# The first scale and shift on 32-column tiles of TensorE, the first norm's scaling and modulation on VectorE

## The chip, the cores and the metric

The program runs on one core of a Trainium2 chip. The metric is the device time of one execution in microseconds. Below, TensorE is PE in the rows (PEld its weight loads), VectorE is DVE, ScalarE is ACT, GpSimd is POOL and SyncE is SP.

## The reference

A two-layer trunk over x of 1024 rows (frames) by 1024 features. Each sub-layer is: RMS norm, adaLN shift and scale made from a vector c, the sub-layer, a gate from c, and the residual sum. Only the beginning matters here:

```python
def rmsnorm(x, w):
    xf = xf * lax.rsqrt(jnp.mean(xf * xf, axis=-1, keepdims=True) + RMS_EPS)
    return xf.astype(x.dtype) * w

def modulate(h, shift, scale):
    return h * (1.0 + scale[:, None, :]) + shift[:, None, :]

# shift, scale, gate (six of 1024 per layer) = silu(c) @ ada_w + ada_b
# layer 0: proj = modulate(rmsnorm(x), shift, scale) @ even_w_in  -> u, q, k, v
```

So before the first projection can start, two products of silu(c) (1024 values) with a 1024x1024 block of `ada_w` must be done, one for the scale and one for the shift.

## The kernel before, in words

The program is written with tile pools, and a scheduler sets the order in which each engine's instructions stand. Each engine then works through its own list from the top, and an instruction that waits holds up all that stand behind it. The parts that the change touches lie in the first 60 us of layer 0 (`even`):

- **Weights** come through `wload` (L74): one transfer of 1 MB into a tile `w` of 128x2048 floats, issued on SP's queue. At the start two rings of two such buffers each serve them, so a fifth load waits until a buffer has been read for the last time.
- **`ada`** (L142) makes one of the six vectors. It loads `ada_w` in four blocks of 256 columns (`h` = 0 to 3), each as eight slices of 128 rows (`k`). Normally VectorE multiplies each slice by its eight values of silu(c) and sums them: one TENSOR_SCALAR (L160) and seven SCALAR_TENSOR_TENSOR (L167) per block give `adacc`, 128x256. TensorE then sums over the partitions, with two matmuls per block against a column of ones (L179). For the first scale, block 2 goes to TensorE as it is: sixteen matmuls with one moving column (L177). VectorE adds the bias (L180), which ends the vector.
- **`norm_S`** (L189) normalizes two tiles of 128 rows at a time: ScalarE squares and sums (L124), VectorE and GpSimd make the reciprocal root (`rm` L131, `rs` L133), the engine `eng` scales the row tile (`xn`, L201), TensorE transposes it in 128x128 pieces (L106). For the first four tiles ScalarE copies the transposed pieces to `pre` (this is `qT`'s memory, L213), since scale and shift aren't there yet.
- **`modulate`** (L217) makes `hm` = x * scale + shift for two slices of features: ScalarE takes one (L223), the engine `eng` the other (L225). Then `split` (L136) makes the high part `hTh` on ScalarE and the rest `hTl` on VectorE (L138, L139). Eight such blocks cover the first 512 rows. They are followed by the other 512 rows, whose `hm` comes straight from PSUM, with VectorE for the second slice.
- **The projections** need for each weight block its own `split` into `wh` and `wl` (two halves each) and then run as three matmuls per product (L240 to L242). They begin when the first blocks of `hTh` are there.
- Behind them, VectorE works in the background on the vectors of the next sub-layers (`gate1` and so on) in the same way.

In the kernel before, `eng` is GpSimd for `xn` of all eight row tiles and for `hm` of the first eight blocks.

Of the kernel before, what the change touches and what calls it, by code (L numbers as in the profile page):

```python
# [9 lines left out]
FT = mybir.dt.float32  # L10
# [13 lines left out]
KD = D // 128  # L24
# [12 lines left out]
class Core:  # L37
# [42 lines left out]
    def consts(self):  # L80
        nc, c = self.nc, self.const
        ji = c.tile([128, 128], I32, name="ji")
        nc.gpsimd.iota(ji, pattern=[[1, 128]], base=0, channel_multiplier=-1)
        self.ident = c.tile([128, 128], FT, name="ident")
        nc.vector.tensor_scalar(self.ident, ji, 0.0, None, op0=OP.is_equal)
        self.ustrict = c.tile([128, 128], BF, name="ustrict")
        nc.vector.tensor_scalar(self.ustrict, ji, 0.0, None, op0=OP.is_gt)
        self.ones_b = c.tile([128, 128], BF, name="ones_b")
        nc.vector.memset(self.ones_b, 1.0)
        self.ones_f = c.tile([128, 128], FT, name="ones_f")  # L90
        nc.vector.memset(self.ones_f, 1.0)
        self.nhalf = c.tile([128, 16], FT, name="nhalf")
        nc.vector.memset(self.nhalf, -0.5)
        self.euler = c.tile([128, 4], FT, name="euler")
        nc.vector.memset(self.euler, math.e)
        self.eps = c.tile([128, 1], FT, name="eps")
        nc.vector.memset(self.eps, 1e-6)
        cr = c.tile([128, KD], FT, name="cr")
        nc.sync.dma_start(cr, self.a["c"][0].rearrange("(k p) -> p k", p=128))
        self.cs = c.tile([128, KD], FT, name="cs")  # L100
        nc.scalar.activation(self.cs, cr, AF.Silu)
        self.mod_d = self.dram.tile([2, 6, D], FT, name="mod_d")
        self.mod = {}
# [37 lines left out]

    def ada(self, i, names, pool, tag, on_pe=((),), pool_eng=False):  # L142

# [3 lines left out]
        for m, nm in enumerate(names):  # L147
# [5 lines left out]
            for h in range(4):  # L153
                w = self.wload(aw[i, :, j * D + h * 256:j * D + (h + 1) * 256], 8)
                if h in on_pe[m % len(on_pe)]:
                    parts.append(w)
                    continue
# [13 lines left out]
            for h, x in enumerate(parts):  # L171
                for q in range(2):
                    qs = slice(q * 128, (q + 1) * 128)
                    p = pc[:, 2 * h + q:2 * h + q + 1]
                    if h in on_pe[m % len(on_pe)]:
                        for k in range(KD):
                            nc.tensor.matmul(p, x[:, k, qs], self.cs[:, k:k + 1], start=(k == 0), stop=(k == KD - 1))  # L177
                    else:
                        nc.tensor.matmul(p, x[:, qs], self.ones_f[:, 0:1], start=True, stop=True)  # L179
            nc.vector.tensor_tensor(o, pc[:, 0:KD], b, op=OP.add)  # L180
# [1804 lines left out]
    def even(self, x_src):  # L1985
# [9 lines left out]
        with self.banks("pse", b=4, a=1, d=1, e=2):  # L1995
# [16 lines left out]
            with tc.tile_pool(name="hT", bufs=1, side="right") as hp, tc.tile_pool(name="wsp", bufs=1, side="right") as wp:  # L2012
                hs = [hp.tile([128, KD, T], FR, name=n) for n in ("hTh", "hTl")]
                with tc.tile_pool(name="nrm", bufs=1, side="left") as np_:
# [13 lines left out]
                    pre = qT[:].rearrange("p h t -> p (h t)").rearrange("p (k t) -> p k t", k=KD)  # L2028
                    self.norm_S(get, None, None, *hs, np_, "ad", range(4), eng=nc.gpsimd, pre=pre)
                    list(self.ada(0, ["scale1", "shift1"], ap, "e", ((2,), ())))  # L2030
                    mod = self.mod["scale1", 0], self.mod["shift1", 0]
                    for h in range(2):
                        ts = slice(256 * h, 256 * h + 256)
                        for k in range(0, KD, 2):
                            self.modulate(pre[:, k:k + 2, ts], k, ts, *mod, *hs, np_, nc.gpsimd)
                    self.norm_S(get, *mod, *hs, np_, "ad", range(4, 8), 512, eng=nc.gpsimd)
                kv = pool(left, "kv", "left")
# [157 lines left out]
```

## Time and profile before

| | us |
|---|---|
| median of 3 runs (3063.31 to 3076.72) | 3067.4 |
| the profiled execution | 3067.3 |
| its span in the trace | 3065.6 |
| around the span | 1.7 |
| TensorE busy | 2658.0 (87%) |
| VectorE busy | 1790.3 (58%) |
| ScalarE busy | 1125.4 (37%) |
| GpSimd busy | 834.4 (27%) |

The shares are means over many stages. What the change is worth is read from the stretch that it touches: the opening up to the first projection at 60 us, the projections up to 288 us that follow it, and what waits for their end.

### The profile page before, as it was taken

To read this page: it belongs to the slowest core of one execution; us is meant where nothing else is said; L and a number is where in the kernel's file an instruction comes from. 1 tells how busy PE (TensorE), PEld (TensorE's weight loads), DVE (VectorE), ACT (ScalarE), POOL (GpSimd) and SP (SyncE) were. 2 spreads that over 40 slices of the span, in tenths; PEclk is the share of its full clock that TensorE was granted. 3 is DMA by queue.
4 is the path that set the end of the run, shared out by engine and by line. 5 is a ranking of instruction groups with operands and counts; after the bars stand their busy time and mean duration, and the time that the engine had idled before them with its cause. 6 is when DMAs were issued, how large, how long until landed. Compare 5 with 4: busy or idle time off the path is not lost. (4 is left out here: it accounts for less than half of the span.)

```text
span 3065.6 us, 39902 instructions
## 1 busy us (share of the span) xinstructions
PE 2658.0 (87%) x14357; PEld 1855.2 (61%) x14357; DVE 1790.3 (58%) x3207; ACT 1125.4 (37%) x1781; POOL 834.4 (27%) x1161
## 2 busy tenths in 40 slices
PE   4987788989699999995899999999978799998991
PEld 4776456647454466662677777777876444566660
DVE  7546999655633467764734555646557434556674
ACT  4311455432222245552433323323233223345451
POOL 5250665224211031101302533354015111121102
PEclk8898699989799999997898977886988799999996
DMA  8747220223588899997645322243333689999996
GB/s 279 177 125 203 58 59 19 86 69 103 214 336 343 348 368 407 377 388 252 262 132 179 106 73 79 74 115 102 103 124 124 235 343 367 367 363 403 382 385 250
DMA packets 344954, 672.82 MB, mean 219 GB/s; under 512 B 118527, under 2 KB 259871, under 8 KB 293040
## 3 DMA queue, kind: packets, MB, share of 16 engines
q1 hardware_dynamic: 272896, 611.23, 54.5%
q10 hardware_dynamic: 56752, 25.41, 3.1%
q0 software_dynamic: 15104, 33.58, 3.0%
q8 instruction: 115, 1.88, 0.3%
q14 instruction: 87, 0.71, 0.1%
HBM read 611.31 MB, written 79.79 MB: 225 GB/s over the span
## 5 line engine op out<-in xcount | busy, mean ns | idle before, releaser
L139 DVE TENSOR_TENSOR wlo<-w,whi 128x1024 fp32r<-128x1024 f32 x384 | 451.1, 1218 | 112.9 <-ACT whi L138 111.4
L138 ACT ACTIVATE whi<-w 128x1024 fp32r<-128x1024 f32 x384 | 390.3, 1054 | 235.9 <-PE ps_g L841 70.5
L240 PE MATMUL ps_b<-hTh,wh 128*128 128x512 f32 x608 | 260.4, 430 | 26.6 <-ACT cc L1388 12.4
L241 PE MATMUL ps_b<-hTl,wh 128*128 128x512 f32 x608 | 257.0, 423 | 0.0
L790 POOL DMA_INDIRECT xg<-h_d,tok x56 | 80.9, 1445 | 639.6 <-PE ps_t L106 613.1
L242 PE MATMUL ps_b<-hTh,wl 128*128 128x512 f32 x608 | 254.9, 419 | 0.0
L849 DVE TENSOR_TENSOR hs<-hs,ps_u 128x512 f32<-128x512 f32 x48 | 32.9, 685 | 263.3 <-PE ps_u L919 212.4
L796 POOL DMA_INDIRECT ye_d<-y,tab x48 | 71.4, 1487 | 422.3 <-DVE y L858 329.4
L167 DVE SCALAR_TENSOR_TENSOR adacc<-w,cs,adacc 128x256 f32<-128x256 f32 x329 | 162.5, 511 | 5.2
L139 DVE TENSOR_TENSOR wl<-w,wh 128x1024 fp32r<-128x1024 f32 x84 | 104.2, 1255 | 100.8 <-ACT wh L138 100.8
L240 PEld LDWEIGHTS ps_b<-hTh,wh 128*128 128x128 f32 x608 | 125.2, 207 | 54.7 <-ACT cc L1388 13.2
L313 DVE TENSOR_TENSOR_SCAN sP<-keep,sP,sbz 128x256 f32<-128x256 f32 (+1 forms) x160 | 134.8, 885 | 22.7 <-ACT keep L300 10.7
L848 ACT ACTIVATE hs<-ps_g 128x512 f32<-128x512 f32 x48 | 28.7, 598 | 325.0 <-PE ps_g L919 244.7
L919 PE MATMUL ps_g<-w,xh 128*64 128x512 f32 x512 | 143.5, 598 | 0.0
L138 ACT ACTIVATE wh<-w 128x1024 fp32r<-128x1024 f32 x84 | 86.3, 1053 | 154.1 <-PE ps_b L241 135.3
L242 PEld LDWEIGHTS ps_b<-hTh,wl 128*128 128x128 f32 x608 | 124.8, 205 | 28.7 <-issue 0.4
L241 PEld LDWEIGHTS ps_b<-hTl,wh 128*128 128x128 f32 x608 | 125.2, 206 | 27.4 <-issue 0.4
L133 POOL TENSOR_TENSOR rs<-rm,nhalf 128x1 f32<-128x1 f32 (+2 forms) x56 | 48.5, 867 | 330.3 <-DVE rm L131 294.3
L919 PE MATMUL ps_u<-w,xh 128*64 128x512 f32 x512 | 137.6, 595 | 0.0
L315 POOL TENSOR_TENSOR sw<-sw,sP 128x512 f32<-128x512 f32 (+1 forms) x80 | 99.2, 1241 | 135.3 <-DVE sP L313 61.9
L928 PE MATMUL ps_y<-w,hh 128*64 128x512 f32 x512 | 122.0, 598 | 2.2 <-ACT hh L923 2.2
L1705 POOL TENSOR_TENSOR T<-N,X 128x60 f32<-128x60 f32 (+24 forms) x248 | 85.8, 346 | 126.5 <-DMA N<-n_d 108.3
(712 smaller groups left out, 6178.9 us busy)
## 6 DMA issues: line engine op xcount, KB each, us to landing
w<-in_moe_w_gate_dram SPq DMA_DIRECT2D x128, 1024.0 KB, 14.6
w<-in_moe_w_up_dram SPq DMA_DIRECT2D x128, 1024.0 KB, 14.6
w<-in_moe_w_down_dram SPq DMA_DIRECT2D x128, 1024.0 KB, 13.4
w<-in_ada_w_dram SPq DMA_DIRECT2D x48, 1024.0 KB, 6.0
w<-in_odd_w_in_dram SPq DMA_DIRECT2D x26, 1024.0 KB, 5.6
cy<-ye_d SPq DMA_DIRECT2D x16, 1024.0 KB, 14.5
cx<-xm_d SPq DMA_DIRECT2D x21, 512.0 KB, 7.2
w<-in_even_w_in_dram SPq DMA_DIRECT2D x8, 1024.0 KB, 8.6
```

The source lines that it names most:

```text
L138: self.nc.scalar.activation(hi, x, AF.Copy)
L139: self.nc.vector.tensor_tensor(lo, x, hi.bitcast(FT), op=OP.subtract)
L167: eng.scalar_tensor_tensor(acc, wk, ck, acc, op0=OP.mult, op1=OP.add)
L240: nc.tensor.matmul(p, a[0], b[0], start=first, stop=False)
L241: nc.tensor.matmul(p, a[0], b[1], start=False, stop=False)
L242: nc.tensor.matmul(p, a[1], b[0], start=False, stop=last)
L313: v.tensor_tensor_scan(P[:, r, 0:n][:, ::-1], keep[:, r, 0:n][:, ::-1], zero.to_broadcast([128, n]), P[:, r, n:n + 1], op0=OP.mult, op1=OP ...
L315: g.tensor_tensor(w[:, :, 0:n], w[:, :, 0:n], P[:, :, 1:n + 1], op=OP.mult)
L790: nc.gpsimd.indirect_dma_start(out=xg, out_offset=None, in_=h_d[:], in_offset=bass.IndirectOffsetOnAxis(ap=tokc, axis=0), bounds_check=T - ...
L919: nc.tensor.matmul(ps[z][r], x[:, 4 * h + k, r], w[z][h][:, k, :], start=(h == 0 and k == 0), stop=(h == 1 and k == 3))
L928: nc.tensor.matmul(py[n][r], ht[:, f, r], w[2][f // 2][:, f % 2, two[n]], start=(f == 0), stop=(f == 3))
L1705: g.tensor_tensor(o, N[:, 0:j, j:j + 1].to_broadcast([128, j, w]), X[:, j:j + 1, c:8].to_broadcast([128, j, w]), op=OP.mult)
```

## The change

Three things are edited. `consts` builds a tile `csz` (128 x 8 x 32, zero but for the first column of each 32, which holds silu(c)) and makes `ident` in place, without the helper tile `ji`. `ada` gets a new path for the first scale and the first shift: for every block, eight matmuls with the 32 columns of `csz` as the stationary side and 256 columns of `w` moving, each into one of four 32-partition strips of a PSUM tile; slices k and k+4 add up in the same strip. ScalarE copies the 128x256 result out (L166 of the changed kernel) and the matmuls with ones follow as before. And `eng` is VectorE for `xn` and for `hm`. Line numbers of the changed kernel are 4 to 7 higher than before.

```diff
+        self.csz = c.tile([128, KD, 32], FT, name="csz")
+        nc.vector.memset(self.csz, 0.0)
+        nc.vector.tensor_copy(self.csz[:, :, 0:1], self.cs[:, :, None])
...
-    def ada(self, i, names, pool, tag, on_pe=((),), pool_eng=False):
+    def ada(self, i, names, pool, tag, on_pe=False, pool_eng=False):
...
-                if h in on_pe[m % len(on_pe)]:
-                    parts.append(w)
+                if on_pe:
+                    pa = self.psum(tag)[:, 0:256]
+                    for k in range(KD):
+                        q = 32 * (k % 4)
+                        nc.tensor.matmul(pa[q:q + 32], self.csz[:, k, :], w[:, k, :], start=(k < 4), stop=(k >= 4), tile_position=(0, q))
+                    acc = pool.tile([128, 256], FT, name="adacc", bufs=4)
+                    nc.scalar.activation(acc, pa, AF.Copy)
+                    parts.append(acc)
                     continue
...
-                    if h in on_pe[m % len(on_pe)]:
-                        for k in range(KD):
-                            nc.tensor.matmul(p, x[:, k, qs], self.cs[:, k:k + 1], start=(k == 0), stop=(k == KD - 1))
-                    else:
-                        nc.tensor.matmul(p, x[:, qs], self.ones_f[:, 0:1], start=True, stop=True)
+                    nc.tensor.matmul(p, x[:, qs], self.ones_f[:, 0:1], start=True, stop=True)
...
-                    self.norm_S(get, None, None, *hs, np_, "ad", range(4), eng=nc.gpsimd, pre=pre)
-                    list(self.ada(0, ["scale1", "shift1"], ap, "e", ((2,), ())))
+                    self.norm_S(get, None, None, *hs, np_, "ad", range(4), eng=nc.vector, pre=pre)
+                    list(self.ada(0, ["scale1", "shift1"], ap, "e", True))
...
-                            self.modulate(pre[:, k:k + 2, ts], k, ts, *mod, *hs, np_, nc.gpsimd)
-                    self.norm_S(get, *mod, *hs, np_, "ad", range(4, 8), 512, eng=nc.gpsimd)
+                            self.modulate(pre[:, k:k + 2, ts], k, ts, *mod, *hs, np_, nc.vector)
+                    self.norm_S(get, *mod, *hs, np_, "ad", range(4, 8), 512, eng=nc.vector)
```

The scheduler reorders the engines around this. On ScalarE, between the last row tile's square and the first `hm`, there stood before:

```order
L124 ACTIVATE xn,ss<-xt 128x1024
L213 ACTIVATE qT<-ps_d 128x2x256
L124 ACTIVATE xn,ss<-xt 128x1024
L138 ACTIVATE wh<-w 128x1024 x4
L223 ACTIVATE hm<-qT,shift_0_282,scale_0_217 128x256 x2
```

and now:

```order
L128 ACTIVATE xn,ss<-xt 128x1024 x3
L115 DMA adac<-in_ada_b_dram 128x8x1
L115 DMA adan<-in_norm_ffn_w_dram 128x8x1
L166 ACTIVATE adacc<-ps_e 128x256 x4
L142 ACTIVATE wh<-w 128x1024 x4
L230 ACTIVATE hm<-qT,shift_0_287,scale_0_219 128x256 x2
```

The four halves `wh` of the first two blocks of `even_w_in` still stand ahead of the first `hm`, and the four copies of the shift's blocks now stand ahead of them.

On VectorE, around the end of the shift, before:

```order
L160 TENSOR_SCALAR adacc<-w,cs 128x256
L167 SCALAR_TENSOR_TENSOR adacc<-w,cs,adacc 128x256 x8
L139 TENSOR_TENSOR wl<-w,wh 128x1024
L167 SCALAR_TENSOR_TENSOR adacc<-w,cs,adacc 128x256
L139 TENSOR_TENSOR wl<-w,wh 128x1024
L180 TENSOR_TENSOR shift_0_282<-ps_e,adac 128x8
L139 TENSOR_TENSOR wl<-w,wh 128x1024 x2
L160 TENSOR_SCALAR adacc<-w,cs 128x256
L139 TENSOR_TENSOR hTl<-hm,hTh 128x2x256
```

and now:

```order
L208 TENSOR_SCALAR xn<-xt,rs_467 128x1024
L143 TENSOR_TENSOR wl<-w,wh 128x1024 x2
L187 TENSOR_TENSOR shift_0_287<-ps_e,adac 128x8
L232 TENSOR_SCALAR hm<-qT,scale_0_219,shift_0_287 128x256 x2
L143 TENSOR_TENSOR wl<-w,wh 128x1024 x2
L171 TENSOR_SCALAR adacc<-w,cs 128x256
L143 TENSOR_TENSOR hTl<-hm,hTh 128x2x256
L178 SCALAR_TENSOR_TENSOR adacc<-w,cs,adacc 128x256
L143 TENSOR_TENSOR hTl<-hm,hTh 128x2x256
L232 TENSOR_SCALAR hm<-qT,scale_0_219,shift_0_287 128x256
```

The shift still stands behind `wl` of the first weight block, the second block's `wl` still behind the shift; the sums for the scale and the shift are gone, and the eight `hm` have come in among the `hTl`.

On TensorE, from the transposes of the third pair of row tiles to the first projection, now:

```order
L164 MATMUL ps_e<-w,csz 32x256 x16
L186 MATMUL ps_e<-ones_f,adacc 128x1 x8
L110 MATMUL ps_a<-ident,xn 128x128
L110 MATMUL ps_d<-ident,xn 128x128
L110 MATMUL ps_a<-ident,xn 128x128 x3
L110 MATMUL ps_d<-ident,xn 128x128 x3
L164 MATMUL ps_e<-w,csz 32x256 x32
L186 MATMUL ps_e<-ones_f,adacc 128x1 x8
L247 MATMUL ps_b<-hTh,wh 128x512 x2
```

The eight matmuls of each of the shift's four blocks stand in one run of 32, with nothing between them, and the ones follow. Apart from this opening and the stretch up to the first projections the lists of the engines are nearly the same, until the recurrent stage of layer 1 (from about 1840 us), where the scheduler interleaves its chains, the second sub-layer and the early output rows in a somewhat different order on all engines.

## Rows read from the trace of the kernel before

**Rows 1.** Busy time by stretch: stretch and length, busy us and instructions of each engine, granted TensorE clock, mean DMA share, GB/s.
```profile
0.00:10.00 10.00, 0.00 (x0) 0.00 (x0) 0.79 (x8) 3.58 (x5) 3.43 (x7) 1.00 0.78 229
10.00:20.00 10.00, 4.20 (x16) 3.00 (x16) 5.83 (x12) 4.78 (x10) 9.23 (x7) 1.00 1.12 355
20.00:30.00 10.00, 7.74 (x35) 7.34 (x36) 9.50 (x22) 2.30 (x4) 5.47 (x4) 1.00 1.07 399
30.00:40.00 10.00, 8.00 (x41) 7.36 (x40) 8.16 (x18) 4.35 (x8) 6.54 (x4) 1.00 1.08 348
40.00:44.00 4.00, 0.34 (x4) 0.25 (x3) 3.82 (x6) 0.24 (x1) 3.90 (x3) 0.55 1.07 350
44.00:48.00 4.00, 1.01 (x4) 0.92 (x4) 3.86 (x10) 3.31 (x4) 0.14 (x1) 0.50 0.40 116
48.00:60.00 12.00, 1.01 (x4) 0.93 (x4) 11.02 (x19) 5.92 (x11) 7.22 (x6) 0.50 0.98 313
60.00:82.00 22.00, 19.69 (x81) 15.76 (x82) 20.92 (x44) 13.01 (x23) 2.50 (x3) 0.82 0.47 155
82.00:288.00 206.00, 191.01 (x843) 156.63 (x841) 115.78 (x329) 35.66 (x38) 67.83 (x181) 0.93 0.65 169
288.00:304.00 16.00, 1.33 (x5) 1.04 (x5) 5.57 (x16) 1.07 (x1) 1.37 (x3) 0.55 0.77 162
1840.00:2280.00 440.00, 414.44 (x3320) 340.14 (x3319) 232.43 (x457) 134.92 (x318) 145.77 (x339) 0.83 0.34 94
```

**Rows 2.** VectorE from 0 to 51.0 us, groups by line: busy us, mean ns of one, idle time before and what ended it.
```profile
L167 DVE SCALAR_TENSOR_TENSOR adacc<-w,cs,adacc 128x256 f32<-128x256 f32 x49 | 28.1, 582 | 1.2
L160 DVE TENSOR_SCALAR adacc<-w,cs 128x256 f32<-128x256 f32 x7 | 3.6, 518 | 1.6 <-DMA w<-in_ada_w_dram 1.6
```

**Rows 3.** VectorE in order of time (start us, length us): the first block's first instruction, the end of the last block, the shift and what follows it.
```profile
14.46 0.73 DVE L160 TENSOR_SCALAR adacc<-w,cs 128x256 f32<-128x256 f32 x1 [1.61 <-DMA w<-in_ada_w_dram]
...
49.22 0.48 DVE L167 SCALAR_TENSOR_TENSOR adacc<-w,cs,adacc 128x256 f32<-128x256 f32 x1
49.61 1.22 DVE L139 TENSOR_TENSOR wl<-w,wh 128x1024 fp32r<-128x1024 f32 x1
50.80 0.17 DVE L180 TENSOR_TENSOR shift<-ps_e,adac 128x8 f32<-128x8 f32 x1
50.88 2.36 DVE L139 TENSOR_TENSOR wl<-w,wh 128x1024 fp32r<-128x1024 f32 x2
```

**Rows 4.** ScalarE in order of time: the halves `wh` of the first two weight blocks, then the first `hm`.
```profile
43.76 2.01 ACT L138 ACTIVATE wh<-w 128x1024 fp32r<-128x1024 f32 x2 [5.64 <-DMA w<-in_even_w_in_dram]
46.45 2.00 ACT L138 ACTIVATE wh<-w 128x1024 fp32r<-128x1024 f32 x2 [0.69 <-DMA w<-in_even_w_in_dram]
51.00 0.60 ACT L223 ACTIVATE hm<-qT,shift,scale 128x256 f32<-128x256 f32 x1 [2.55 <-DVE shift L180]
```

**Rows 5.** SP's queue: the issues of those two blocks, and what SP waited for in the first 60 us (us in total, times, longest).
```profile
34.81 0.37 SPq L77 DMA_DIRECT2D w<-in_even_w_in_dram  x1
39.71 0.37 SPq L77 DMA_DIRECT2D w<-in_even_w_in_dram  x1
...
SPq L77 <- DVE adacc L167: 16.6, 4, 6.0
```

**Rows 6.** The moved work: on GpSimd `xn` (0 to 51 us) and `hm` (51 to 64 us), groups by line; then the nearest rows of such work on VectorE (ns min/median/max): `xn`'s form in the second norm, and a TENSOR_SCALAR of 128x256 out of SBUF.
```profile
L201 POOL TENSOR_SCALAR xn<-xt,rs 128x1024 f32<-128x1024 f32 x8 | 23.4, 2932 | 0.6
L225 POOL TENSOR_SCALAR hm<-qT,scale,shift 128x256 f32<-128x256 f32 x8 | 9.7, 1220 | 9.9 <-DVE shift L180 6.9 <-DVE hTl L139 3.0
L201 DVE TENSOR_SCALAR cy<-cx,rs x8: 732/750/1285, 1431.1 to 1498.8; 128x1024 f32<-128x1024 f32 x8
L160 DVE TENSOR_SCALAR adacc<-w,cs x47: 260/353/1480, 14.5 to 613.6; 128x256 f32<-128x256 f32 x47
```

**Rows 7.** TensorE, plain float32 matmuls, which appear as two records each: full width with 512 moving columns (L681); two 64-column tiles side by side with 512 moving columns (L919); weight loads of 32 columns (L1093, ns min/median/max).
```profile
690.16 3.68 PE L681 MATMUL ps_e<-w,gl 128*128 128x512 f32 x8
847.22 3.65 PE L919 MATMUL ps_g<-w,xh 128*64 128x512 f32 x16
L1093 PEld LDWEIGHTS ps_b<-q_w,r_o x64: 106/110/178, 718.5 to 2392.8; 128*32 128x32 f32 x64
```

**Rows 8.** TensorE's pace in order of time: four transposes in the opening and later; the first projection matmuls; the same some us later.
```profile
33.53 1.09 PE L106 MATMUL ps_a<-ident,xn 128*128 128x128 f32 x4
60.34 1.22 PE L240 MATMUL ps_b<-hTh,wh 128*128 128x512 f32 x2 [9.58 <-ACT hTh L138]
61.78 0.63 PE L242 MATMUL ps_b<-hTh,wl 128*128 128x512 f32 x1
62.21 0.63 PE L240 MATMUL ps_b<-hTh,wh 128*128 128x512 f32 x1
66.66 0.39 PE L240 MATMUL ps_b<-hTh,wh 128*128 128x512 f32 x1
66.89 0.39 PE L241 MATMUL ps_b<-hTl,wh 128*128 128x512 f32 x1
69.39 0.60 PE L106 MATMUL ps_a<-ident,xn 128*128 128x128 f32 x4
```

**Rows 9.** VectorE from 51 to 83 us, groups by line, as rows 2.
```profile
L167 DVE SCALAR_TENSOR_TENSOR adacc<-w,cs,adacc 128x256 f32<-128x256 f32 x28 | 13.4, 490 | 0.2
L139 DVE TENSOR_TENSOR hTl<-hm,hTh 128x512 fp32r<-128x512 f32 x16 | 11.3, 714 | 1.2 <-ACT hTh L138 1.2
L225 DVE TENSOR_SCALAR hm<-ps_a,scale,shift 128x256 f32<-128x256 f32 x4 | 2.1, 534 | 0.0
```

More of the change, by code (lines that the diff above doesn't have):

```diff
@@ L81, in consts @@
         nc, c = self.nc, self.const
-        ji = c.tile([128, 128], I32, name="ji")
+        self.ident = c.tile([128, 128], FT, name="ident")
+        ji = self.ident[:].bitcast(I32)
         nc.gpsimd.iota(ji, pattern=[[1, 128]], base=0, channel_multiplier=-1)
-        self.ident = c.tile([128, 128], FT, name="ident")
-        nc.vector.tensor_scalar(self.ident, ji, 0.0, None, op0=OP.is_equal)
         self.ustrict = c.tile([128, 128], BF, name="ustrict")
         nc.vector.tensor_scalar(self.ustrict, ji, 0.0, None, op0=OP.is_gt)
+        nc.vector.tensor_scalar(self.ident, ji, 0.0, None, op0=OP.is_equal)
         self.ones_b = c.tile([128, 128], BF, name="ones_b")
```

## The prediction

> **What bounds the opening.** I read the busy time by stretch first. Look at the DMA share in the first rows: from 10 to 44 us it stands at 1.07 to 1.12 with 348 to 399 GB/s, while VectorE is busy for 9.5 of 10 us from 20 to 30 us [rows 1]. So two things run at their limit at once, the transfers and VectorE, and the question is which of them ends last. The order of time on VectorE tells when: it takes the first block of `ada_w` at 14.46 us, finishes its last sum at 49.70, and the shift is written at 50.80 [rows 3]. What waits for it is ScalarE: its first `hm` starts at 51.00, after 2.55 us of idleness that the shift ended [rows 4]. This idle time is the most important number of the case. Ahead of it ScalarE made the four `wh` of the first two weight blocks, which waited for their transfers; the last was done at 48.45. So the transfers are only 2.55 us behind VectorE as a bound on this start.
>
> Then the modulation runs through ScalarE, GpSimd and VectorE, and the first projection matmul starts at 60.34 us, released by `hTh` [rows 8]. Up to 82 us VectorE is nearly full (20.92 of 22 us), from there to 288 us TensorE is (191 of 206), and the 16 us that follow have almost no TensorE work, because the loads of the next stage come only after the projections [rows 1]. Whatever shortens the opening should therefore move all that follows by about the same amount, no more.
>
> **What is taken off VectorE.** The 49 + 7 instructions of seven blocks, 28.1 + 3.6 us of busy time [rows 2]. It looks like the gain, and is not: at its end stands a wait of 2.55 us, and beneath it the transfers. Four MiB of x, eight of `ada_w` and two of `even_w_in` (14 x 1.049 = 14.7 MB) stand ahead of the first `hm` in ScalarE's list, also in the changed one. The rates of the first rows give 2.3 + 3.6 + 4.0 + 3.5 + 1.4 = 14.7 MB by 44 us [rows 1]: the queue was never idle by much, so the second weight block can't land before about 44 us; before, it was there at 46.45. With 2.0 us for its two `wh`, `hm` starts between 46.0 and 48.45 instead of 51.00. SP waited 16.6 us for VectorE to give buffers back, and issued the second weight block 4.9 us after the first [rows 5]; some of the 2.4 us between the two ends may come from that. Since the DMA rows show no hole before 44 us I take the near end, **-2.55 us** (bounds -5.0 and, if TensorE is late, 0 or a loss, below).
>
> **What is put on TensorE.** 64 matmuls, 128 records, each with 256 columns moving. A full-width record with 512 columns takes 3.68/8, about 0.44 us from start to start, so one with 256 about 0.22; with 64-column tiles side by side 16 records of the same 512 columns fit in 3.65 us, 0.22 each, so two tiles do overlap [rows 7]. No row shows four 32-column tiles. Per block that makes 16 x 0.22 = 3.5 us without any overlap, 1.8 in pairs, 0.9 in fours. In the opening TensorE runs slower: four transposes take 1.09 us there and 0.60 later, although the rows print a granted clock of 1.00; the first projection matmuls stand 0.43 us apart and from about 64 us on 0.23 [rows 8], with the granted clock going from 0.50, which is 1.2 GHz, to 2.4 GHz after some 4 us of dense matmuls. At the slow pace a block costs up to 6.6, 3.3 or 1.7 us. The blocks arrive one per 2.6 to 3.0 us (1.05 MB at 350 to 399 GB/s), and some 30 transposes and the ones (about 7 + 3.5 us at the slow pace) lie between. For `hm` not to slip, the last copy has to be done 4 us before 51.0; with 14.5 us as the first block's arrival that is met up to (51.0 - 4.0 - 0.6 - 14.5 - 10.5)/8 = **2.7 us per block**. Fours pass it at any pace, pairs at 2.4 GHz pass it, pairs at 1.2 GHz miss it by 0.6 x 8 = 5 us. I take that it passes: overlap is shown, and an engine that falls behind its loads works without a pause, which is what preceded the rise of the clock at 64 us.
>
> The Trainium skill speaks against it ("TensorE: Matmul & The Clock Gate", Part 3, The mechanism): weight loads overlap running matmuls only when the row group differs, and tiles that differ in columns alone share all their rows. By that rule every record here would carry its own weight load, 0.11 us in the nearest row [rows 7]. The 64-column rows do not bear it out, since their 16 records leave no room for one; for 32 columns no run here shows it.
>
> **What moves from GpSimd to VectorE.** `xn`: eight of 2.93 us on GpSimd against 0.75 us in the same form on VectorE [rows 6], 6 us in a stretch that has just lost 31.7. It lets the transposes start sooner, but x arrives with the transfers; nothing on the path. `hm`: eight of 1.22 us against 0.26 to 0.35 us each, 2.1 to 2.8 us [rows 6]. These do cost something: they fall in the stretch where VectorE is full. Two of them fit ahead of the second block's `wl`, which waits for `wh` until 48.45; the other six are 1.6 to 2.1 us. In return VectorE waited 1.2 us for `hTh` [rows 9], partly GpSimd's doing. So VectorE, which has its two `wl` behind it about 2.4 us sooner, ends its modulation by 82 us only 0.3 to 2.0 us sooner. TensorE idled 2.3 us between 60 and 82 us [rows 1], so its lead is somewhere between this and 2.55; I take 2.3.
>
> **The rest.** Eight copies on ScalarE (0.6 us each by the 128x256 `hm` of rows 4) fall in stretches where it is busy for 2.3 to 4.8 of 10 us [rows 1]; only the last is near the path, and is in the bound above. `csz` and `ident` are ready long before the first row tile. SP's list no longer mixes x with `ada_w`, with the same bytes. GpSimd has nothing behind `hm` that could use its 33 us.
>
> **Sum.** 3067.3 us of the profiled execution (0.1 under the median of the runs) less 2.3 is **3065 us**. Against a measurement that can tell about 0.5%, or 15 us, this is no change.
>
> **Rivals.**
> - *TensorE is the new bound* (slower). If the 32-column tiles do not overlap, the opening is TensorE's: 128 records at 0.41 us (0.22 x 0.43/0.23) are 53 us, with 10.5 of other work and 4.6 behind them `hm` starts at 14.5 + 68 = 82 us, 31 late: 3098. At 2.4 GHz it would be 14.5 + 28 + 5 + 4.6 = 52, 3068; pairs at 1.2 GHz, 3072. It decides from 2.7 us per block. For it: no row with four tiles, the slow pace in the opening. Against it: the pairs of rows 7. As a case I price it between, at 3085 us. Chance 0.12. The Trainium skill's rule on weight loads, above, belongs to this rival: with it the 128 records would take 128 x (0.22 + 0.11) = 42 us at 2.4 GHz, and the time would be 3082.
> - *The full lead* (faster). Buffers come free sooner, the second weight block lands at 44, VectorE without GpSimd beside it is quicker (its sums took 582 ns in the opening, 490 after [rows 2, 9]), and the lead is 5 us or some more: 3060 us. For it: SP's waits. Against it: the DMA rows. Chance 0.18.
> - *The order of layer 1.* From 1840 to 2280 us the lists differ. TensorE is busy there for 414 of 440 us at a mean clock of 0.83 [rows 1], so 26 us of idleness and the clock can be won or lost in part. With half of that idleness as the bound, +-13 us on top of the forecast: 3052 or 3078. Nothing in the rows gives a sign. Chance 0.08 for each side beyond 8 us.
> - *Nothing comes of it*: the stretch from 60 to 82 us takes the lead back. That is 3067 and lies inside the forecast.
>
> **The numbers.** The forecast, a lead of 0 to 4 us, has 0.54. The range has to hold half of the layer 1 cases on either side and the bounds of the opening, and the runs of the kernel before lie between 3063 and 3077: 3050 to 3079, which leaves out most of the first rival and the far ends of the order. Faster by over 0.5% (under 3052) needs the full lead and a good order: 0.10. Slower by over 0.5% (over 3083) needs the unoverlapped tiles or a bad order with a late TensorE: 0.09. In between 0.81.
>
> **What would show it.** Right: the shift done by about 47 us, `hm` on ScalarE released no longer by the shift but directly behind `wh`, at 46 to 48.5 us; the DMA share still above 1 up to 44 us; a block on TensorE under 2.7 us; first projection matmul at about 57 to 58 us, end of the projections near 286 us; no `xn` and no `hm` on GpSimd. Wrong: `hm` waiting for `adacc` copies, blocks of 3 us or more back to back on TensorE, or a first matmul later than 60 us; a difference over 10 us in 1840 to 2280 us would say that the order decides and not the opening.

## The result and the profile after

The changed kernel takes **3087.3 us** (median of 18 runs, 3075.1 to 3095.7) against 3067.6 us before (18 runs, 3061.1 to 3076.7): a ratio of **1.0060, 95% interval 1.0050 to 1.0070**. The prediction said 3065 us and no change that can be told, with a range of 3050 to 3079, and put slower by over 0.5% at 0.09. It is slower by a little more than that, some 19 us, and lies above the range. The profiled execution of the changed kernel took 3093.4 us, with a span of 3091.2.

Start where the change was made. Busy time by stretch in the changed kernel, columns as in [rows 1]:

```profile
10.00:20.00 10.00, 7.53 (x62) 5.29 (x62) 2.54 (x6) 7.31 (x15) 1.63 (x3) 1.00 1.11 353
20.00:30.00 10.00, 7.99 (x57) 5.93 (x56) 2.42 (x8) 6.01 (x12) 1.63 (x3) 0.66 1.06 401
30.00:40.00 10.00, 6.49 (x55) 2.36 (x57) 1.17 (x3) 1.15 (x3) 0.54 (x1) 0.50 1.12 358
40.00:44.00 4.00, 4.00 (x27) 2.79 (x22) 0.47 (x1) 1.94 (x3) 0.00 (x0) 0.50 1.09 386
44.00:48.00 4.00, 1.28 (x6) 1.19 (x6) 3.96 (x7) 3.23 (x5) 0.00 (x0) 0.50 1.09 386
48.00:60.00 12.00, 3.77 (x8) 2.57 (x9) 12.00 (x28) 7.83 (x15) 0.00 (x0) 0.50 0.66 213
60.00:82.00 22.00, 19.77 (x90) 16.06 (x90) 17.39 (x40) 9.81 (x17) 0.00 (x0) 0.91 0.58 190
82.00:288.00 206.00, 185.62 (x828) 151.64 (x826) 113.97 (x323) 35.19 (x38) 68.02 (x181) 0.95 0.66 165
1840.00:2280.00 440.00, 402.27 (x3273) 328.44 (x3272) 228.52 (x457) 134.86 (x316) 144.59 (x340) 0.83 0.34 94
```

VectorE has become mostly idle up to 40 us, and the DMA share now stays above 1 without a break up to 48 us: in [rows 1] it was 0.40 from 44 to 48. TensorE's granted clock is at 0.50 (1.2 GHz) from 30 to 60 us, where it stood at 1.00 up to 40 us in [rows 1].

TensorE in order of time, the blocks on 32-column tiles, the ones behind them and the first projection matmul:

```profile
18.09 1.07 PE L164 MATMUL ps_e<-w,csz 128*32 128x256 f32 x16
36.84 1.94 PE L164 MATMUL ps_e<-w,csz 128*32 128x256 f32 x16 [1.18 <-DMA w<-in_ada_w_dram]
39.84 1.94 PE L164 MATMUL ps_e<-w,csz 128*32 128x256 f32 x16 [1.06 <-DMA w<-in_ada_w_dram]
41.70 3.57 PE L186 MATMUL ps_e<-ones_f,adacc 128*128 128x1 f32 x16
55.77 1.22 PE L247 MATMUL ps_b<-hTh,wh 128*128 128x512 f32 x2 [10.49 <-ACT hTh L142]
```

A block costs 1.07 us at the full clock and 1.94 us at half of it: four tiles run side by side. The last four blocks each wait for their transfer, so TensorE keeps pace. The first projection matmul starts at 55.8 us, 4.6 us earlier than in [rows 8]. VectorE around the shift:

```profile
43.53 2.36 DVE L143 TENSOR_TENSOR wl<-w,wh 128x1024 fp32r<-128x1024 f32 x2 [11.64 <-ACT wh L142]
45.81 0.16 DVE L187 TENSOR_TENSOR shift<-ps_e,adac 128x8 f32<-128x8 f32 x1
46.00 0.73 DVE L232 TENSOR_SCALAR hm<-qT,scale,shift 128x256 f32<-128x256 f32 x2
```

and ScalarE's halves `wh` of the second weight block and the first `hm`:

```profile
45.21 1.06 ACT L142 ACTIVATE wh<-w 128x1024 fp32r<-128x1024 f32 x1 [0.77 <-DMA w<-in_even_w_in_dram]
46.17 1.04 ACT L142 ACTIVATE wh<-w 128x1024 fp32r<-128x1024 f32 x1
47.12 1.08 ACT L230 ACTIVATE hm<-qT,shift,scale 128x256 f32<-128x256 f32 x2
```

The shift is written 5.0 us earlier than in [rows 3], and `hm` stands directly behind `wh`, as forecast; the 2.55 us of [rows 4] are gone. So the opening went well, and the loss must lie later. Layer 1 shows it. The first gather of layer 1's experts (GpSimd) and the last expert matmuls (TensorE), in the kernel before:

```profile
2400.84 1.17 POOL L790 DMA_INDIRECT xg<-h_d,tok  x1 [11.76 <-DVE tok L1148]
...
2997.49 7.09 PE L928 MATMUL ps_y<-w,hh 128*64 128x512 f32 x32 [0.69 <-ACT hh L923]
```

and in the changed one:

```profile
2417.40 1.18 POOL L797 DMA_INDIRECT xg<-h_d,tok  x1 [11.68 <-DVE tok L1155]
...
3023.99 7.09 PE L935 MATMUL ps_y<-w,hh 128*64 128x512 f32 x32 [0.69 <-ACT hh L930]
```

At the first gather of layer 0 the two stand 1.4 us apart (812.2 and 813.5 us). At that of layer 1 they are 16.6 us apart, at the last expert matmul 26.5. So the time is lost in layer 1, which the change doesn't touch: about 15 us in its recurrent stage ("mixer" below, from gather to gather) and 10 in its experts. What TensorE waited for from 2000 to 2290 us (us in total, times, longest), before:

```profile
PE ps_o L681 <- DVE om L684: 5.4, 2, 2.8
PE ps_b L106 <- ACT my L1523: 1.3, 2, 0.8
```

and after:

```profile
PE ps_o L688 <- DVE om L691: 13.0, 4, 7.2
PE ps_b L110 <- ACT my L1530: 6.6, 2, 4.8
PE ps_a L1662 <- DVE C L1666: 3.4, 1, 3.4
```

`om` belongs to the early output rows, `my` and `C` to the chains that the scheduler interleaves with them. Same instructions, other places in the lists. That the places are the cause is so far only a reading; the experiments test it.

### The profile page after: what moved, and what is told of

The parts are those of the page before. It is cut to its first block, busy times and chain, and to the rows that moved or that the text cites. A ratio compares the mean times of both kernels' runs of the same rounds, so it can differ in the third digit from the quotient of the medians.

```text
span 3091.2 us, 40058 instructions
## 1 busy us (share of the span) xinstructions
PE 2667.6 (86%) x14457; PEld 1853.2 (60%) x14457; DVE 1767.3 (57%) x3169; ACT 1129.4 (37%) x1789; POOL 799.7 (26%) x1145
## 5 line engine op out<-in xcount | busy, mean ns | idle before, releaser
L797 POOL DMA_INDIRECT xg<-h_d,tok x56 | 89.9, 1606 | 644.1 <-PE ps_t L110 611.5
L803 POOL DMA_INDIRECT ye_d<-y,tab x48 | 61.5, 1281 | 429.3 <-DVE y L865 345.9
L178 DVE SCALAR_TENSOR_TENSOR adacc<-w,cs,adacc 128x256 f32<-128x256 f32 x280 | 133.7, 499 | 3.9
```

What stands on the lines that cost most here:

```text
L178: eng.scalar_tensor_tensor(acc, wk, ck, acc, op0=OP.mult, op1=OP.add)
L797: nc.gpsimd.indirect_dma_start(out=xg, out_offset=None, in_=h_d[:], in_offset=bass.IndirectOffsetOnAxis(ap=tokc, axis=0), bounds_check=T - ...
```

## The experiments

**Means.** A kernel can be given the order of another one: `pin` adds dependencies of order alone (no semaphore, no wait) between successive instructions of each engine, from a table (`ORDER`, counted from instruction `FIRST`). It covers 9484 instructions, layer 1's mixer and its experts, and computes nothing. Instruction for instruction each engine then follows the list of the kernel that the table was taken from.

```diff
+    def pin(self):
+        table = json.loads(zlib.decompress(base64.b85decode("".join(ORDER))))
+        ins = {int(x.name[2:]): x for x in self.nc.cur_bb.bb.instructions if x.name[2:].isdigit()}
+        kind = mybir.DependencyInfo(mybir.DependencyClass.NoSync, mybir.DependencyReason.DATA)
+        for steps in table.values():
+            n, last = FIRST, None
+            for s in steps:
+                n += s
+                if last is not None:
+                    self.tc.add_manual_dep(ins[n], ins[last].name, kind, reason="order")
+                last = n
...
+        if i == 1:
+            self.pin()
         n_ov = nc.values_load(...
```

All ratios below are to the kernel before, timed beside the run, with 95% intervals.

**1. The change with layer 1 in the order of before** (`x1`): the edit above, in the changed kernel.

> The changed kernel, with nothing changed in what it computes, but all five engines' lists from the start of layer 1 to the end of its dense experts (the second large block of the program, 9484 instructions) held in the order that the kernel before has there. The opening and layer 0 stand as in the changed kernel. Theory A, the 20 us were lost because the scheduler wrote layer 1 in another order: 3062 to 3071 us, ratio to the kernel before 0.998 to 1.001, and the matched instructions of layer 1 no longer fall behind by 13 us between 1840 and 2360 us nor by another 10 us up to 3040 us. Rival B, the loss comes from what the opening sets going (buffers and transfers in another phase through all that follows): 3083 to 3091 us, ratio 1.005 to 1.008, as the changed kernel. Rival C, half each: about 3077.

Measured: 3070.3 us, 1.0006 (0.9994 to 1.0017). The whole loss is gone, with the whole change in place.

**2. The kernel before with layer 1 in the order of after** (`x2`): the edit above in the kernel before, with the other table.

> The kernel before, its opening and layer 0 as they were, but the lists of all five engines in layer 1 and its dense experts held in the order that the changed kernel has there. Theory A (order of layer 1): 3083 to 3092 us, ratio 1.005 to 1.008, with no part of the change in it. Rival B (phase set by the opening): 3064 to 3071 us, ratio 0.999 to 1.001. Rival C: about 3077.

Measured: 3087.1 us, 1.0058 (1.0043 to 1.0073). The loss is there with nothing of the change. These two together show the cause: the order of the lists in layer 1.

**3. The changed kernel again** (`e0`), unedited, as a second profile.

> The changed kernel once more, for a second profiled execution of it. Theory A and rival B alike: 3083 to 3093 us, ratio 1.005 to 1.007. What it tells is which of the shifts between the two profiles come back: the lead of 4 us lost at 230 to 245 us, the 13 us between 2040 and 2360 us and the 10 us between 2640 and 3040 us. If the 10 us are a matter of single runs, they are missing here and the profiled execution is 10 us shorter than the first one's 3093.4.

Measured: 3084.4 us, 1.0052 (1.0036 to 1.0069); first layer 1 gather at 2407.7 us, last expert matmul at 3019.4. The first profile lay at the slow end of its runs; the sizes below are therefore means over runs.

**4 and 5. One stage alone.** The kernel before, with the lists of after for the mixer alone (`x4`) and for the experts alone (`x5`): the edit of 1 with a table cut at the experts' first instructions.

> The kernel before, with the lists of layer 1's mixer alone (up to the routing of its last row tile, about 1420 to 2390 us) in the order of the changed kernel, and the dense experts of layer 1 in the order that before has. Theory A1, the loss lies in the mixer, where TensorE waits for the early output rows (om) and for the SSD's my: ratio 1.003 to 1.005, 3077 to 3083 us, 10 to 14 us later by 2300 us, and the distance stays the same up to the end. Rival A2, the loss is one of the experts' lists, and the mixer's delay is taken back there since the weight stream sets the experts' pace: 1.000 to 1.001, under 3072 us.

> The kernel before, with the mixer of layer 1 as in before and the lists of its dense experts alone (from about 2390 us) in the order of the changed kernel; SyncE's list is the same in both there. Theory A1 with the second term, 8 us lost between 2560 and 2720 us by a longer hole in the weight stream: ratio 1.002 to 1.003, 3074 to 3078 us. Rival A2, all of the loss: 1.005 to 1.007. Rival A3, the experts' lists cost nothing and their 8 us only follow from the mixer's end being late: 0.999 to 1.001.

Measured: 3079.4 us, 1.0034 (1.0021 to 1.0047), and 3077.2 us, 1.0030 (1.0017 to 1.0043). Within their intervals the parts add up to the 1.0058 of both. The profiles agree (us; mixer is gather to gather, experts from layer 1's gather to the end of the last expert matmul):

| | lists of mixer, experts | mixer | experts |
|---|---|---|---|
| before | before, before | 1588.7 | 603.7 |
| `x1` | before, before | 1586.2 | 603.2 |
| after | after, after | 1603.9 | 613.7 |
| `e0` | after, after | 1597.1 | 611.7 |
| `x2` | after, after | 1599.8 | 611.4 |
| `x4` | after, before | 1593.6 | 601.7 |
| `x5` | before, after | 1588.2 | 613.7 |

Over all profiled runs the mixer takes 1588.8 us with the list of before (11 runs, 1586 to 1595) and 1598.6 with that of after (4 runs, 1594 to 1604), the experts 603.2 (11 runs, 601 to 605) and 612.3 (5 runs, 611 to 614): **+9.8 and +9.1 us**. Holding a list costs nothing that the stages show: in before's own order, held, the mixer takes 1588.2 us (`x5`) and the experts 601.7 (`x4`), as against 1588.7 and 603.7 where the scheduler wrote the same order.

The waits shown above come back as well. From 2000 to 2290 us TensorE waits for `om` for 4.1 to 5.5 us in each of the eleven runs with the mixer's list of before and for 11.6 to 14.1 us in each of the four with that of after; its waits for other engines in this stretch sum to 24.8 us in the mean of the eleven and to 37.0 in that of the four. From gather to gather TensorE idles for 162.7 and 174.8 us, and its busy time is the same within 3 us. So in the mixer the time is lost in waiting.

How can an order cost time where every instruction is the same? TensorE's 64-column groups in the experts of `x5` (lines are those of `x5`; busy us, mean ns of one):

```profile
L935 PE MATMUL ps_g<-w,xh 128*64 128x512 f32 x256 | 73.4, 599 | 0.0
L935 PE MATMUL ps_u<-w,xh 128*64 128x512 f32 x256 | 69.8, 594 | 0.0
L944 PE MATMUL ps_y<-w,hh 128*64 128x512 f32 x256 | 62.9, 598 | 1.1 <-ACT hh L939 1.1
```

and in the kernel before:

```profile
L919 PE MATMUL ps_g<-w,xh 128*64 128x512 f32 x256 | 71.2, 597 | 0.0
L919 PE MATMUL ps_u<-w,xh 128*64 128x512 f32 x256 | 68.4, 595 | 0.0
L928 PE MATMUL ps_y<-w,hh 128*64 128x512 f32 x256 | 61.0, 598 | 1.1 <-ACT hh L923 1.1
```

Count and mean length are nearly the same, the busy time is 5.5 us more over the three: the tiles lie side by side less of the time. For the stage as a whole, columns as in [rows 1], `x5`:

```profile
2402.30:3015.96 613.66, 576.36 (x2483) 338.35 (x2483) 319.88 (x379) 248.17 (x291) 77.49 (x55) 0.98 0.92 359
```

and the kernel before:

```profile
2400.84:3004.58 603.74, 569.95 (x2483) 337.71 (x2483) 318.17 (x379) 247.15 (x291) 76.77 (x55) 0.98 0.91 365
```

So here both rose, TensorE's busy time and its idle time. In the means of the eleven and the five runs these are 4.8 and 4.3 of the 9.1 us. Which places in the list break the tiles up was not tried.

**6. The early output rows put back** (`x8`): `x4`, but the matmuls of the early rows stand behind the same TensorE instruction as in the kernel before, and their multiplications and sums and SyncE's issues are left to the scheduler (only the table changes). The theory was that these matmuls, placed too early, hold up TensorE until VectorE has made `om` and so emptied their PSUM tile.

> As x4 (before's kernel, mixer of layer 1 in the changed kernel's order), but the matmuls of the early output rows each held behind the same TensorE instruction as in before; their multiplications, sums and SyncE's issues of the mixer are left to the scheduler. Theory A1a, the early rows' place is what costs: the waits of TensorE for om and my shrink from 16 us to under 9, ratio 1.000 to 1.002, 5 us or more under x4. Rival A1b, it is the interleaving of the recurrent chains as a whole: as x4, within 3 us.

Measured: 3084.4 us, 1.0042 (1.0025 to 1.0059), no better than `x4`. TensorE's waits from 2000 to 2290 us in `x8`:

```profile
PE ps_o L684 <- DVE om L687: 10.4, 3, 8.0
PE ps_k L1789 <- DVE P L1785: 6.5, 2, 6.0
PE ps_b L109 <- ACT my L1541: 5.7, 4, 2.0
```

The wait for `om` stands at 10.4 us, as against 11.6 in `x4`, and one for `P`, of the interleaved chains as well, has grown by its side (2.0 in `x4`). Putting these matmuls back neither shortened the stage (1597.3 us, 1593.6 in `x4`) nor took the waits away. The place of these matmuls alone isn't the cause in the mixer, then; whether the waits for `om` are, this run can't tell, since they stayed.

**7. Where does the opening's lead go?** With layer 1 held, the change should have shown 4 us, and `x1` shows none (1.0006, 2 us faster at the most by its interval). `y3` is `x1` with one piece of the background vectors moved from the sixth slot to the fourth:

```diff
-                    for _ in range((0, 1, 1, 2, 2, 2, 0, 0)[n]):
+                    for _ in range((0, 1, 1, 3, 2, 1, 0, 0)[n]):
```

> The changed kernel with layer 1 in the order of before (as x1), and one of the background vectors begun one weight block earlier in the projections (0, 1, 1, 3, 2, 1 per block in place of 0, 1, 1, 2, 2, 2), which puts five loads of ada_w ahead of the first load of the next stage's weights and four behind it, in place of four and five. Theory L1, the opening's lead of 4 us is lost at 190 to 245 us because TensorE stands behind sums of vectors that wait for their transfers (12.5 us of waiting there): 3 to 6 us under x1, 3063 to 3067 us, ratio 0.997 to 0.999, and the end of the projections 3 us or more earlier than the 286 us of both kernels. Rival L2, the lead is lost to the start of the next stage (its loads) or to chance: as x1, 3068 to 3072 us.

Measured: 3072.3 us, 1.0011 (0.9999 to 1.0023). No gain: TensorE's waits for `adacc` from 60 to 290 us are 13.6 us, as against 8.6 to 12.5 in the four runs with the projections of after (after, `e0`, `x1`, and `z1` of experiment 9) and 8.4 to 11.0 in the seven with those of before (before, `x2`, `x4`, `x5`, `x8`, and `t0` and `z2` of experiment 9).

Where the lead goes can be read from the profiles of these four and seven runs, by numbering the projection matmuls in order of time. The first one comes 4.2 us sooner with the changed opening, the 300th (about 150 us) and the 480th (about 196 us) 2.8 us sooner, the 600th (241 us) and all that follow 0.2 us sooner. The last one, in after and in the kernel before:

```profile
283.77 0.39 PE L249 MATMUL ps_b<-wh,hTl 128*128 128x512 f32 x1
```

```profile
283.68 0.39 PE L242 MATMUL ps_b<-wh,hTl 128*128 128x512 f32 x1
```

So a third of the lead is gone by 100 us, and the rest is lost between 229 and 241 us. In that stretch TensorE waits once more for `adacc` in three of the four profiles, for 3.6 to 5.3 us, in after like this:

```profile
236.38 0.61 PE L186 MATMUL ps_e<-ones_f,adacc 128*128 128x1 f32 x4 [3.55 <-DVE adacc L178]
```

Of the seven, four have no such wait there and the others one of 0.8 to 2.3 us.

**8. The matmuls with ones later** (`w1`: `x1` with layer 0's list held as well, but four pairs of them moved behind 16, 16, 8 and 16 further TensorE instructions; `w2`: the same in the kernel before). `w3` and `w4` are these two with two `wl` on VectorE moved ahead of sums that waited for `ada_w`, and the fourth pair 36 places later. Tables alone change.

> The changed kernel with layer 1 in before's order (as x1), and on TensorE four pairs of matmuls with ones (the sums of background vectors that it waited for at 193.7, 208.5, 224.1 and 236.4 us, 12.5 us in all) moved 16, 16, 8 and 16 places later among the projection matmuls; everything else in layer 0 in the changed kernel's order, but for the bias sums and issues that follow these pairs. Theory L1, these waits take the opening's lead: waiting there under 5 us, end of the projections (last matmul before 300 us) at 276 to 281 us in place of 286, and the whole 4 to 9 us under x1, 3061 to 3066 us, ratio 0.997 to 0.999. Rival L2, the wait only changes its place (TensorE then waits for wh and wl of the next weight block, whose load stands behind ada_w in SyncE's list): as x1, 3068 to 3072 us.

> The kernel before, with the same four pairs moved by the same numbers of places (the pairs that it waits for at 198.6, 212.3 and 228.1 us, 9.1 us in all, and the one behind). Theory L1: it gains as well, but less, since it waits less there: 3062 to 3067 us; and w1 is 2 to 4 us faster than this, the opening's lead carried through. Rival L2: 3067 to 3070 us, and w1 no faster.

> As w1 (changed kernel, layer 1 in before's order, pairs with ones later), with two more moves: on VectorE the two halves wl of the weight block for which TensorE waited 10.1 us in w1 stand ahead of the background sums that waited for ada_w, and the fourth pair with ones is 36 places later in place of 16. Theory L1, the projections wait only because of the places in these lists: the waits of TensorE for adacc and wl in 190 to 250 us fall from 18 us (w1) and 9 us (x1) to under 6, the last projection matmul comes at 277 to 282 us, and the whole at 3060 to 3066 us, ratio 0.997 to 0.999. Rival L3, the transfers of ada_w set the pace whatever the lists say (each new place finds the next wait): last projection matmul at 284 to 288, 3068 to 3074 us.

> The same moves in the kernel before. Theory L1: 3062 to 3068 us, and w3 2 to 4 us faster than this, the opening's lead carried through. Rival L3: 3067 to 3074 us, w3 no faster.

Measured: 1.0022 (1.0010 to 1.0033), 1.0023 (1.0012 to 1.0034), 1.0024 (1.0011 to 1.0037) and 1.0027 (1.0014 to 1.0041). All lose 7 to 9 us, more than any of the theories and rivals allowed (at most 3074 us, and they take 3074.6 to 3076.0), and in either pair the change gains nothing over before that can be told (1.1 and 0.5 us). Layer 0's list held without these moves was not run, so what holding it costs isn't separated from what the moves cost. TensorE in `w1`:

```profile
210.32 1.01 PE L189 MATMUL ps_e<-ones_f,adacc 128*128 128x1 f32 x4 [8.15 <-DVE adacc L181]
...
238.66 0.79 PE L251 MATMUL ps_b<-wl,hTh 128*128 128x512 f32 x1 [10.10 <-DVE wl L146]
```

Before, the longest wait of this kind there was

```profile
228.07 0.95 PE L179 MATMUL ps_e<-ones_f,adacc 128*128 128x1 f32 x4 [4.53 <-DVE adacc L167]
```

and in `w1` VectorE itself stands still ahead of that `wl`:

```profile
232.66 0.35 DVE L174 TENSOR_SCALAR adacc<-w,cs 128x256 f32<-128x256 f32 x1 [10.83 <-DMA w<-in_ada_w_dram]
...
237.38 1.22 DVE L146 TENSOR_TENSOR wl<-w,wh 128x1024 fp32r<-128x1024 f32 x1
```

So the moved wait came back longer. With `wl` moved ahead of the sums (`w3`) it still does:

```profile
210.54 1.02 PE L189 MATMUL ps_e<-ones_f,adacc 128*128 128x1 f32 x4 [8.80 <-DVE adacc L181]
...
236.99 0.80 PE L251 MATMUL ps_b<-wl,hTh 128*128 128x512 f32 x1 [8.03 <-DVE wl L146]
```

What sets the pace of this chain from 200 to 245 us stays open: each wait that was taken away was followed by another.

**9. A transfer of single words in the experts.** In the kernel before, the rate falls to 64 GB/s from 2700 to 2710 us, where a table of slots is written in 4-byte pieces (16 KB in 38.8 us from its issue at 2669.0 us). If a list's place against this hole made the difference, a table in rows should remove it (`t0` in before, `z2` in `x5`, `z1` in `x1`):

```diff
-        nc.scalar.dma_start(tab_d.rearrange("(b s) o -> s (b o)", s=128), tab)
+        nc.scalar.dma_start(tab_d.rearrange("(s b) o -> s (b o)", s=128), tab)
...
-                nc.sync.dma_start(ic, tab_d[ds(b * 128, 128), :])
+                nc.sync.dma_start(ic, tab_d.rearrange("(s b) o -> s (b o)", s=128)[:, ds(b, 1)])
```

> The kernel before with one edit: the overflow table, which goes to memory beside the experts' weights as 4096 single elements of 4 bytes in both layers, is stored as 128 rows of 32 elements, and its reader takes a column of that. All lists stand as in before. Theory S, the small packets hold up the weight stream, which sets the experts' pace: the hole of 64 GB/s at 2700 to 2710 us and the one of 190 GB/s at 1100 to 1110 us are gone, ratio 0.994 to 0.998 (3 to 9 us a layer). Rival P, TensorE is as close to its limit there (77 of 80 us busy): 0.999 to 1.001.

> As x5 (before's kernel, the lists of layer 1's experts alone in the changed kernel's order), and the table stored in rows as in t0. Theory S, the order of the experts costs 0.3% because it lets the table's small packets fall among the weights at a worse moment: the distance to t0 shrinks from the 9 us between x5 and before to 3 us or less. Rival S2, the order costs by itself (TensorE waits for wlo and hs, buffers come free later): 7 to 10 us over t0, as before.

> The changed kernel with layer 1 in before's order (as x1) and the table stored in rows. Theory S: 6 to 18 us under x1, 3052 to 3064 us, ratio 0.994 to 0.998, under both kernels. Rival P: as x1, 3067 to 3072 us.

Measured: 1.0000 (0.9992 to 1.0009), 1.0025 (1.0015 to 1.0034) and 1.0009 (0.9997 to 1.0020). Busy time by stretch in the kernel before:

```profile
2700.00:2710.00 10.00, 10.00 (x45) 8.10 (x44) 9.04 (x9) 7.64 (x8) 0.28 (x1) 1.00 0.77 64
...
2730.00:2740.00 10.00, 10.00 (x47) 3.40 (x47) 0.00 (x0) 0.60 (x1) 0.00 (x0) 1.00 1.01 406
```

and in `t0`:

```profile
2700.00:2710.00 10.00, 9.26 (x45) 7.35 (x44) 8.75 (x10) 6.31 (x8) 1.54 (x1) 1.00 1.01 416
...
2730.00:2740.00 10.00, 10.00 (x42) 5.62 (x40) 0.00 (x0) 0.00 (x0) 0.69 (x1) 1.00 0.77 285
```

The hole is gone and a shallower one has come, 273 to 308 GB/s from 2720 to 2750 us. TensorE gains nothing by that: from 2690 to 2760 us it is busy for 66.4 us in both. The theory falls, and `z2` shows that the experts' order costs its 8 us with the table in rows too (its lowest rate from 2660 to 2760 us is 228 GB/s).

**10. Half of the change, lists left to the scheduler.** `v2`: the kernel before with `eng` = VectorE alone. `v1`: the changed kernel with `eng` = GpSimd, so the tiles on TensorE alone.

```diff
-                    self.norm_S(get, None, None, *hs, np_, "ad", range(4), eng=nc.gpsimd, pre=pre)
+                    self.norm_S(get, None, None, *hs, np_, "ad", range(4), eng=nc.vector, pre=pre)
...
-                            self.modulate(pre[:, k:k + 2, ts], k, ts, *mod, *hs, np_, nc.gpsimd)
-                    self.norm_S(get, *mod, *hs, np_, "ad", range(4, 8), 512, eng=nc.gpsimd)
+                            self.modulate(pre[:, k:k + 2, ts], k, ts, *mod, *hs, np_, nc.vector)
+                    self.norm_S(get, *mod, *hs, np_, "ad", range(4, 8), 512, eng=nc.vector)
```

This is `v2`; `v1` is its reverse in the changed kernel.

> One part of the change alone: the kernel before with xn and hm of the first norm on VectorE, the sums for scale and shift on VectorE as in before, and the scheduler left to write all lists. Its opening gives the VectorE 6 us more of xn and 2 of hm ahead of the projections, so the first projection matmul comes at 60 to 66 us; layer 1 comes in a third order. Theory A, that order is a draw of its own around the changed kernel's rather than before's: 3072 to 3092 us, more than the opening's 0 to 4 us late. Rival D, only the change as a whole upsets the order and this draw is like before's: 3066 to 3073 us.

> The other part of the change alone: scale and shift on 32-column tiles of TensorE, while xn and hm of the first norm stay on GpSimd; the scheduler writes all lists, so layer 1 comes in a fourth order. Its opening should be as early as the changed kernel's or 1 to 2 us later (hm on GpSimd at 1.22 us each). Theory A, the order is a draw: anything from 3066 to 3092 us, set by layer 1, while the stretch up to 286 us is within 3 us of the changed kernel's. Rival E, the 20 us belong to the TensorE part: 3083 us or more.

Measured: 3076.7 us, 1.0026 (1.0014 to 1.0039), and 3090.5 us, 1.0075 (1.0061 to 1.0090). With both halves it is 1.0060, so the halves don't add up: each edit gets lists of its own. Theory A has the total of `v1` right and the place wrong: its loss lies ahead of layer 1. There TensorE waits once for 12.1 us for `wl`, the last projection matmul comes at 294.0 us (283.8 in after), the first layer 0 gather at 829.3, 16 late; the mixer takes 1589.8 us, as with the list of before, and the experts 606.7. In `v2` most of the loss stands in the experts, 607.6 us instead of 603; its first projection matmul comes at 58.1 us, sooner than the 60 to 66 that were expected. Of the new orders that were run, three were written by the scheduler for the whole program (after, `v1`, `v2`) and four have a part moved by hand (`x8`, `y3`, `w1`, `w3`). None is faster than before, and all but `y3` are slower by their intervals.

## Why the prediction was wrong, point by point

- **What bounds the opening**: right. The transfers were the second bound, and they are the bound now; the near end of -2.55 us was taken, and what came lies between the ends: -3.9 us for `hm` on ScalarE (51.00 to 47.12), -4.6 at the first projection matmul. The reason given for the near end, that the queue had no hole before 44 us, overlooked that the hole lay from 44 to 48 us, with a share of 0.40 [rows 1]: that stretch now runs at 1.09. The rival "full lead" was nearer here.
- **TensorE's blocks under 2.7 us**: right, 1.07 and 1.94 us. Overlap fourfold was an estimate from pairs, and holds at either clock. The rule of the Trainium skill ("TensorE: Matmul & The Clock Gate", Part 3, The mechanism), that weight loads overlap running matmuls only where the row group differs, is not borne out here. The weight loads of a block, which all use the same rows, lie on one another in time and beside the block's matmuls:

```profile
30.96 1.93 PE L164 MATMUL ps_e<-w,csz 128*32 128x256 f32 x16 [0.45 <-DMA w<-in_ada_w_dram]
30.93 0.23 PEld L164 LDWEIGHTS ps_e<-w,csz 128*32 128x32 f32 x8 [0.82 <-issue]
31.36 0.23 PEld L164 LDWEIGHTS ps_e<-w,csz 128*32 128x32 f32 x4 [0.20 <-issue]
31.79 0.22 PEld L164 LDWEIGHTS ps_e<-w,csz 128*32 128x32 f32 x4 [0.20 <-issue]
```

  Sixteen loads take 0.68 us in all, and the last eight of them begin while the block of 1.93 us is running. Four abreast the records alone take about 1.6 us at this clock (4 x 0.41, the prediction's estimate for one), so with the loads on top of them the block would take 2.3. The rival "TensorE is the new bound" and its 3082 fall.
- **What moves to VectorE**: right but for a size. `xn` costs 6.0 us in all (753 ns each) and lies in idle time; `hm` costs 3.2 us (407 ns each), where 2.1 to 2.8 were forecast; from 60 to 82 us VectorE is busy for 17.4 us, not 20.9.
- **A lead of 2.3 us**: near what is read at 288 us, but by luck. Over the profiled runs with either opening (four and seven), the first projection matmul comes at 55.7 us instead of 59.8, the last one at 282.3 instead of 282.4, the last TensorE instruction before the pause at 288 us (attention scores, which wait for VectorE) at 286.0 instead of 288.1, the first layer 0 gather at 812.0 instead of 813.2. So 4.2 us shrink to 0.2 at the end of the projections; the 2.1 and 1.2 behind it lie within what runs of one kind scatter there (2.4 to 5.3 us). The sentence "whatever shortens the opening should therefore move all that follows by about the same amount" failed in this: TensorE stands behind the ones, these behind VectorE's background sums, and these behind `ada_w`. The waits for `adacc` up to 290 us are 11.5 us in the mean of the four and 9.3 in that of the seven, so they take about 2 of the 4 us. That this chain takes the lead back is a reading of the waits; the runs of 7 and 8 failed to free it.
- **The order of layer 1** is the step that failed. It was a rival with "+-13 us", 0.08 for each side, limited to 1840 to 2280 us. Three things in it were wrong. It stopped at 2280 us, while the experts' lists differ too; their 9.1 us were in no term. It was put as symmetric ("nothing in the rows gives a sign"), while, of the other orders that were run, none gained and all but one lost; with three whole draws of the scheduler among them, that slower is the rule is likely but not shown. And it was treated as a tail, though the lists were known to differ: it had no place in the sum. The sum by the terms measured: 3067.3 - 1.2 + 9.8 + 9.1 = 3085, against 3087.3. The 9.8 us lie within the rival's +-13; it is the 9.1 beyond its end, and the missing term in the sum, that put the time above the range.
- **What would show it**: the text named a difference of over 10 us in 1840 to 2280 us as the sign that the order decides. TensorE's busy time there fell from 414.4 to 402.3 us, and `x1` and `x2` show that it does.

What stays open: which places in the mixer's lists cost the 9.8 us (shown are the stage's total and that TensorE waits more there; the matmuls of the early rows alone are not it), which places in the experts' lists break the overlap and lengthen the idle time, and what sets the pace from 229 to 241 us.

## What to carry to other kernels

Where a scheduler writes the lists, an edit at the start can change every list behind it; compare the lists over the whole program, give each stage in which they differ a price of its own, and let that price stand in the sum, towards slower if the redrawn lists that were tried all lose, as nearly all did here. To measure what an edit itself is worth, hold the lists behind it fixed, as in the first experiment: here that turned 1.0060 into 1.0006. A shortened opening is worth only what the next chain that waits for transfers lets through.

## What the runs showed of the hardware

- Four 32-column tiles with float32 data run side by side: 16 records of 256 moving columns in 1.07 us at the full granted clock and in 1.94 us at 0.50, where one after another would take 3.5 us at the full clock by an estimate from [rows 7]. Weight loads of the same rows lie on one another: 16 in 0.68 us.
- How much two 64-column tiles overlap changes with the order of the lists: 768 records of nearly the same mean length had 200.6 us of busy time in one order and 206.1 in another (before and `x5`).
- Taking away a stretch of 10 us at 64 GB/s, in which a table was written in 4-byte pieces, gained nothing measurable where TensorE was full through it (1.0000, 0.9992 to 1.0009).
